# Attention slots in another order: scores one slot sooner, one queued item a slot, quotients ahead of copies and weight casts

## The chip, the core and the metric

The kernel runs on one core of a Trainium2 chip. The time is the device time of one execution, in microseconds (us). Five engines each work through their own list of instructions in order and signal one another by semaphores: TensorE (PE in the profile, its weight loads as PEld), VectorE (DVE), ScalarE (ACT), GpSimd (POOL) and SyncE (SP), which here only issues DMAs.

## The reference

A decoder trunk of two layers over 512 tokens of width 1024, in float32: a recurrent layer, a dense feed-forward layer (SwiGLU), an attention layer, a second SwiGLU. Only the attention layer matters here:

```python
def attention_layer(x, norm_g, w_qkv, q_norm, k_norm, w_out):
    b, l, _ = x.shape
    h = rmsnorm(x, norm_g)
    qkv = (h @ w_qkv).reshape(b, l, 3, ATT_HEADS, ATT_HEAD_DIM)
    pos = jnp.arange(l, dtype=jnp.float32)
    q = partial_rope(rmsnorm(qkv[:, :, 0], q_norm), pos) * (ATT_HEAD_DIM ** -0.5)
    k = partial_rope(rmsnorm(qkv[:, :, 1], k_norm), pos)
    v = qkv[:, :, 2]
...
    for window, dilation in DILATED_PATTERNS:
        o_i, m_i, d_i = dilated_window_attention(q, k, v, window, dilation)
...
    wts = jnp.stack(dens) * jnp.exp(m_all - jnp.max(m_all, axis=0, keepdims=True))
    o = jnp.sum(wts[..., None] * jnp.stack(outs), axis=0) / jnp.sum(wts, axis=0)[..., None]
    o = o.astype(x.dtype).reshape(b, l, ATT_WIDTH)
    return x + o @ w_out
```

There are 16 heads of 64 channels. The three window patterns, merged by their softmax denominators, amount to one softmax over scores to which the logarithm of how many patterns see the key is added; the kernel holds that table in `lnc`.

## The kernel before

Every float32 matrix is split into two parts, `hi` (a cast on ScalarE, line 89) and `lo` (the remainder, a subtraction on VectorE, line 90), and a product is three matmuls. A weight block of 128 x 1024 comes by one DMA on SP's queue into one of three raw buffers, is split by `weight_emit`, and is used two blocks later.

The attention layer is written as two streams that one hand-written order weaves together (`manual_schedule`: the four compute engines keep the order in which the code emits). The first stream is a list of `pieces`, each six matmuls of 512 columns or twelve of 256, some 1.4 us of TensorE. A group g of four heads has 16 pieces for queries and keys (`qk_pieces`) and 8 for values (`v_pieces`); then come 16 pieces of the output projection for each half of the heads (`ao_pieces`). The last four query and key pieces of a group are followed by `finish_a` (copy out of PSUM and square on ScalarE), `finish_b` (sum of squares on VectorE, a power on GpSimd), `finish_c` (scaling), `finish_d` and `finish_e` (rotary part).

The second stream is the attention of eight pairs of heads, 0 to 7, each in twelve slots, 0 to 11. For a head, `turn(h, b)` transposes a block of probabilities into PSUM and splits it (`ph` on ScalarE, `pl` on VectorE), and `values(h, b)` multiplies it into the one output buffer `po`; b is 0, 1, 2. After `values(h, 2)` ScalarE copies half of `po` to `bot` and VectorE adds both halves into `o` (`add`), which frees `po`; after a pair's second head `o` is split for the output projection. For the next pair, `pair_T` transposes queries and keys (`qk_hi`, `qk_lo`), and `scores(p + 1, b)` makes three sets of scores. Each set is reduced with a custom VectorE instruction (line 885), goes through the exponential on ScalarE (line 886), then `quotients`: a reciprocal of the sums on VectorE (line 891) and a product per block on GpSimd (line 893). `turn(h, 0)` reads all blocks of a head's probabilities, so it needs the quotients of all three sets. Transposes, scores and probabilities share three PSUM buffers (tag `pm`); pieces have four of their own (`pa`).

After the steps of a slot, `fill_in` runs the pieces of that slot. Inside a piece the weight split of a later block and the copy out of PSUM are emitted at once. After each piece `tick` runs those finishing steps that are due by a count of pieces. Only then come the functions in `after_piece`: `quotients` and `add`.

## Time and profile before

| | us |
|---|---|
| median of 3 runs | 1377.83 (1377.36 to 1377.85) |
| profiled execution | 1378.62 |
| its span | 1376.8 |
| attention stage, first projection to last output piece | 718 to 1017 |
| pair 0 begins | 772.9 |
| pairs 1 to 7 begin their first full turn | 804.4, 833.3, 864.6, 894.1, 925.3, 945.7, 970.4 |
| last values of pair 7 | 984.2 |

TensorE is busy for 97% of the span. A matmul's row gives its start and a modelled duration, longer than the distance to the next start, since matmuls overlap. A wait stands in brackets at the end of a row, with the instruction that ended it. The granted clock is the share of TensorE's full speed that the throttle let through.

### The profile page before, as it was taken

How to read it: one execution, taken by the hardware profiler on the slowest of the kernel's cores; microseconds unless marked ns; L12 is line 12 of the kernel's file. 1: busy time of each engine (PE TensorE's matmuls, PEld its weight loads, DVE VectorE, ACT ScalarE, POOL GpSimd, SP SyncE). 2: the span in 40 equal slices, each digit the busy share in tenths (PEclk: the TensorE clock that was granted, in tenths of full speed). 3: DMA queues.
4: the chain of work that ended last, by engine and by line, in shares of the span. 5: the costliest groups of instructions: out<-in, count | busy, mean ns of one | idle time of the engine just before them, and what ended most of it. 6: DMA issues, size and time to landing. Idle time of an engine off the chain costs nothing.

```text
span 1376.8 us, 16001 instructions
## 1 busy us (share of the span) xinstructions
PE 1331.5 (97%) x6314; PEld 1091.1 (79%) x6314; DVE 781.3 (57%) x1264; ACT 553.9 (40%) x818; POOL 75.9 (6%) x94
## 2 busy tenths in 40 slices
PE   8999989999999999999999989888899999999998
PEld 6877767788888888888888877676688888888887
DVE  7877799875544344444465566575564444444442
ACT  6643857443323223223343646464452222222221
POOL 0000000000000000000002314131000000000000
PEclk9999999999999999999999999998999999999999
DMA  6322223532333333333232211110123323333322
GB/s 234 108 92 77 93 77 107 152 93 92 92 101 99 92 96 99 94 97 104 82 102 92 62 53 56 49 59 31 46 92 95 104 92 94 102 88 100 107 88 81
DMA packets 38555, 126.53 MB, mean 92 GB/s; under 512 B 4288, under 2 KB 5056, under 8 KB 38352
## 3 DMA queue, kind: packets, MB, share of 16 engines
q1 hardware_dynamic: 38480, 125.51, 29.5%
q8 instruction: 49, 0.80, 0.2%
q14 instruction: 26, 0.21, 0.1%
HBM read 123.36 MB, written 2.13 MB: 91 GB/s over the span
## 4 chain that ended last, share of the span: by engine, by line
PE 88%; DVE 5%; ACT 5%; issue 1%; POOL 0%; DMA 0%; SPq 0%; ACTq 0%; POOLq 0%; DVEq 0%
PE ps_pr L118 24%; PE ps_pr L119 24%; PE ps_pr L120 23%; PE ps_qkv L763 2%; PE ps_qkv L764 2%; PE ps_qkv L765 2%; ACT s L886 1%; PE ps_pT L901 1%; DVE wl L90 1%; PE ps_ao L118 1%; ACT wh L89 1%; PE ps_ao L119 1%; PE ps_ao L120 1%; PE ps_s L874 1%; PE ps_o L916 1%
## 5 line engine op out<-in xcount | busy, mean ns | idle before, releaser
L89 ACT CAST wh<-wr 128x1024 fp32r<-128x1024 f32 (+2 forms) x223 | 227.9, 1023 | 589.2 <-PE ps_pr L120 386.3
L118 PE MATMUL ps_pr<-xh,wl 128*128 128x512 f32 x1056 | 416.9, 395 | 12.4 <-DVE wl L90 12.0
L119 PE MATMUL ps_pr<-xl,wh 128*128 128x512 f32 x1056 | 414.8, 393 | 0.0
L120 PE MATMUL ps_pr<-xh,wh 128*128 128x512 f32 x1056 | 413.6, 392 | 0.0
L90 DVE TENSOR_TENSOR wl<-wr,wh 128x1024 fp32r<-128x1024 f32 (+2 forms) x223 | 265.1, 1190 | 86.1 <-ACT wh L89 85.3
L118 PEld LDWEIGHTS ps_pr<-xh,wl 128*128 128x128 f32 x1056 | 199.6, 189 | 55.4 <-DVE wl L90 12.9
L119 PEld LDWEIGHTS ps_pr<-xl,wh 128*128 128x128 f32 x1056 | 199.6, 189 | 42.9 <-DVE xl L193 1.3
L120 PEld LDWEIGHTS ps_pr<-xh,wh 128*128 128x128 f32 x1056 | 199.6, 189 | 42.4 <-issue 0.7
L118 PE MATMUL ps_pr<-ah,wl 128*128 128x512 f32 x352 | 136.9, 389 | 0.0
L119 PE MATMUL ps_pr<-al,wh 128*128 128x512 f32 x352 | 136.9, 389 | 0.0
L120 PE MATMUL ps_pr<-ah,wh 128*128 128x512 f32 x352 | 136.9, 389 | 0.0
L672 DVE TENSOR_TENSOR tu<-ps_pr,nrb 128x512 f32<-128x512 f32 x44 | 30.4, 691 | 130.7 <-PE ps_pr L120 130.7
L680 DVE TENSOR_TENSOR x<-ps_pr,x 128x512 f32<-128x512 f32 x48 | 33.2, 692 | 122.6 <-PE ps_pr L120 122.6
L670 DVE TENSOR_TENSOR tg<-ps_pr,nrb 128x512 f32<-128x512 f32 x44 | 30.4, 691 | 94.0 <-PE ps_pr L120 94.0
L120 PEld LDWEIGHTS ps_pr<-ah,wh 128*128 128x128 f32 x352 | 66.1, 188 | 13.8
L119 PEld LDWEIGHTS ps_pr<-al,wh 128*128 128x128 f32 x352 | 66.1, 188 | 13.7
L118 PEld LDWEIGHTS ps_pr<-ah,wl 128*128 128x128 f32 x352 | 66.1, 188 | 13.6
L886 ACT ACTIVATE s<-s,m 128x512 f32<-128x512 f32 (+3 forms) x64 | 35.4, 554 | 55.6 <-DVE m L885 42.1
L763 PE MATMUL ps_qkv<-wh,xl 128*128 128x512 f32 x128 | 54.8, 428 | 0.0
L764 PE MATMUL ps_qkv<-wl,xh 128*128 128x512 f32 x128 | 51.2, 400 | 0.0
L765 PE MATMUL ps_qkv<-wh,xh 128*128 128x512 f32 x128 | 51.1, 400 | 0.0
L901 PE MATMUL ps_pT<-cst,s 128*128 128x128 f32 x160 | 30.1, 303 | 19.3 <-POOL s L893 19.2
(230 smaller groups left out, 1633.6 us busy)
## 6 DMA issues: line engine op xcount, KB each, us to landing
wr<-in_w_gu SPq DMA_DIRECT2D x88, 512.0 KB, 3.5
wr<-in_w_in SPq DMA_DIRECT2D x35, 512.0 KB, 3.5
wr<-in_w_dn SPq DMA_DIRECT2D x32, 448.0 KB, 3.3
wr<-in_w_qkv SPq DMA_DIRECT2D x24, 512.0 KB, 3.5
wr<-in_w_out SPq DMA_DIRECT2D x16, 512.0 KB, 3.5
wr<-in_w_dn SPq DMA_DIRECT2D x16, 512.0 KB, 3.5
x<-in_xT SPq DMA_DIRECT2D x16, 256.0 KB, 3.5
bcs<-csd SPq DMA_DIRECT2D x16, 256.0 KB, 4.3
```

The lines of the kernel that those rows point to most:

```text
L89: S.copy(hi, src)
L90: V.tensor_tensor(out=lo, in0=src, in1=hi.bitcast(F32), op=ALU.subtract)
L118: mm(ps, lhsT=wl[ws], rhs=xh[xs], start=start, stop=False)
L119: mm(ps, lhsT=wh[ws], rhs=xl[xs], start=False, stop=False)
L120: mm(ps, lhsT=wh[ws], rhs=xh[xs], start=False, stop=stop)
L670: V.tensor_tensor(out=tg, in0=pg, in1=rb, op=ALU.mult)
L680: V.tensor_tensor(out=x[m], in0=ps, in1=x[m], op=ALU.add)
L763: mm(pss[t], lhsT=xl[:, ts_], rhs=wh[:, cols], start=(k == 0), stop=False)
L764: mm(pss[t], lhsT=xh[:, ts_], rhs=wl[:, cols], start=False, stop=False)
L765: mm(pss[t], lhsT=xh[:, ts_], rhs=wh[:, cols], start=False, stop=(k == KD - 1))
L886: S.activation(s, s, AF.Exp, scale=-1.0, bias=m[:, 0, u:u + 1], accum_out=m[:, 1, u:u + 1])
L901: nc.tensor.transpose(ps[:, c + (i - j) * P:c + (i - j + 1) * P], prob[h, i][:, j * P:(j + 1) * P], ident)
```

## The change

The pieces now lie in one order with all of a group's 24 pieces added before an even pair. `slot_end` replaces `fill_in`: after each piece it runs one function of `queue` (finishing steps, now one at a time, whatever the count), then the functions of `behind` (`quotients`, `add`), then those of `last` (weight splits and copies out of PSUM, which pieces now only register). A slot without a piece does the last three steps alone. The steps of a pair are given by `head_steps`: each values stands two slots behind its turn, the next pair's scores stand in slots 5, 7 and 9 (6, 8 and 10 before), and a pair's last values move into slot 0 of the next pair, in front of its first turn. The pieces given to pairs 0 to 7 are 12, 12, 12, 12, 10, 5, 4, 4 (12, 12, 12, 12, 12, 4, 5, 4 before), 40 instead of 36 pieces run before pair 0, and one is left after pair 7 instead of three.

```diff
-        after_piece = []
-
-        def later(n, f):
-
-            queue.append([n, f])
-
-        def tick():
-            for e in queue:
-                e[0] -= 1
-            due = [e for e in queue if e[0] <= 0]
-            queue[:] = [e for e in queue if e[0] > 0]
-            for _, f in due:
-                f()
+        behind, last = [], []
...
                 if t == 2:
-                    weight_emit(i + AHEAD)
+                    last.append(lambda: weight_emit(i + AHEAD))
                 if kp == 3:
-                    finish_a(t)
+                    last.append(lambda: finish_a(t))
...
-                later(2, lambda: finish_b(t, sq))
-                later(6, lambda: finish_c(t))
+                queue.append(lambda: finish_b(t, sq))
                 if t == NT - 1:
-                    later(7, finish_d)
-                    later(8, finish_e)
+                    for u in range(NT):
+                        queue.append(lambda u=u: finish_c(u))
+                    queue.extend(finish_d + [finish_e])
...
-            after_piece.append(quotients)
+            behind.append(quotients)
...
-            after_piece.append(add)
+            behind.append(add)
...
-        def fill_in(n=1):
-            for _ in range(min(n, len(pieces))):
-                pieces.pop(0)()
-                tick()
-            ready = after_piece[:]
-            after_piece.clear()
-            for f in ready:
+        def slot_end(n=1):
+
+            for _ in range(max(n, 1)):
+                if n:
+                    pieces.pop(0)()
+                if queue:
+                    queue.pop(0)()
+                for fs in (behind, last):
+                    ready = fs[:]
+                    fs.clear()
+                    for f in ready:
+                        f()
+
+        def head_steps(p):
+
+            ha, hb = 2 * p, 2 * p + 1
+            steps = [
+                [lambda: turn(ha, 0)],
+                [lambda: pair_T(p + 1, 0)],
+                [lambda: values(ha, 0), lambda: turn(ha, 1)],
+                [lambda: pair_T(p + 1, 1)],
+                [lambda: values(ha, 1), lambda: turn(ha, 2)],
+                [lambda: scores(p + 1, 0)],
+                [lambda: values(ha, 2), lambda: turn(hb, 0)],
+                [lambda: scores(p + 1, 1)],
+                [lambda: values(hb, 0), lambda: turn(hb, 1)],
+                [lambda: scores(p + 1, 2)],
+                [lambda: values(hb, 1), lambda: turn(hb, 2)],
+                [],
+            ]
+            if p == 7:
+                steps = [fs if k % 2 == 0 else [] for k, fs in enumerate(steps)]
+            if p > 0:
+                steps[0].insert(0, lambda: values(ha - 1, 2))
+            return steps
...
-                n = [12, 12, 12, 12, 12, 4, 5, 4][p]
-                nxt = p < 7
-                ha, hb = 2 * p, 2 * p + 1
-                steps = [
-                    [lambda: turn(ha, 0)],
-                    [lambda: turn(ha, 1)] + ([lambda: pair_T(p + 1, 0)] if nxt else []),
-                    [lambda: values(ha, 0), lambda: turn(ha, 2)],
-                    [lambda: values(ha, 1)] + ([lambda: pair_T(p + 1, 1)] if nxt else []),
-                    [lambda: values(ha, 2)],
-                    [lambda: turn(hb, 0)],
-                    [lambda: scores(p + 1, 0)] if nxt else [],
-                    [lambda: values(hb, 0), lambda: turn(hb, 1)],
-                    [lambda: scores(p + 1, 1)] if nxt else [],
-                    [lambda: values(hb, 1), lambda: turn(hb, 2)],
-                    [lambda: scores(p + 1, 2)] if nxt else [],
-                    [lambda: values(hb, 2)],
-                ]
-                for k, fs in enumerate(steps):
+                n = (12, 12, 12, 12, 10, 5, 4, 4)[p]
+                for k, fs in enumerate(head_steps(p)):
                     for f in fs:
                         f()
-                    fill_in(n * (k + 1) // 12 - n * k // 12)
-            fill_in(len(pieces))
+                    slot_end(n * (k + 1) // 12 - n * k // 12)
+            values(15, 2)
+            slot_end(len(pieces))
```

Three places show what this does to the lists of the engines. The first is VectorE at the end of pair 0, from the reduction of the next pair's last scores (`s,m<-ps_s`) to its reciprocal (`m<-m`); `wl` is the low part of a weight, `v` a value block, `q<-rc,rs` the rotary sum, `pl` the low part of turned probabilities. Before:

```order
L885 ISA s_6157,m_6156<-ps_s_6148,cst_82 128x256
L885 ISA m_6156 128x1
L885 ISA s_6160,m_6156<-ps_s_6149,cst_82 128x256
L885 ISA m_6156 128x1
L90 TENSOR_TENSOR wl133_6177<-wr133_6175,wh133_6176 128x1024
L838 SCALAR_TENSOR_TENSOR v_6181<-ps_v_6023,nrt_5431,v_6181 128x4x64
L807 TENSOR_TENSOR q_5685<-rc_6144,rs2_6145 128x32x8
L808 TENSOR_TENSOR q_5685<-rc_6144,rs2_6145 128x32x8
L891 RECIPROCAL m_6156<-m_6156 128x2
L838 SCALAR_TENSOR_TENSOR v_6204<-ps_v_6058,nrt_5431,v_6204 128x4x64
```

Now:

```order
L878 ISA s_6197,m_6196<-ps_s_6188,cst_82 128x256
L878 ISA m_6196 128x1
L878 ISA s_6200,m_6196<-ps_s_6189,cst_82 128x256
L878 ISA m_6196 128x1
L884 RECIPROCAL m_6196<-m_6196 128x2
L90 TENSOR_TENSOR pl_6220<-ps_pT_6216,ph_6219 128x256
L90 TENSOR_TENSOR wl134_6231<-wr134_6229,wh134_6230 128x1024
```

The weight's low part, a value block and the rotary sums stood between the reduction and the reciprocal; nothing stands there now.

The second is ScalarE at the end of pair 1, around the exponentials of the last scores (128x256 x2); `q` and `qsq` are `finish_a`, `ph` and `wh` are casts of probabilities and of a weight, `bot` the copy out of `po`. Before:

```order
L89 CAST ph_6417<-ps_pT_6414 128x256
L886 ACTIVATE s_6436,m_6435<-s_6436,m_6435 128x256
L886 ACTIVATE s_6439,m_6435<-s_6439,m_6435 128x256
L89 CAST wh136_6449<-wr136_6448 128x1024
L924 COPY bot_6302<-ps_o_6356 64x512
L89 CAST xh9_6467<-o_6301 128x512
L89 CAST ph_6476<-ps_pT_6471 128x512
L774 ACTIVATE q_6225<-ps_qkv_6221,nrt_5431 128x512
L776 ACTIVATE qsq_6487<-q_6225 128x512
```

Now:

```order
L764 ACTIVATE qsq_6441<-q_6179 128x512
L879 ACTIVATE s_6452,m_6451<-s_6452,m_6451 128x256
L879 ACTIVATE s_6455,m_6451<-s_6455,m_6451 128x256
L762 ACTIVATE q_6179<-ps_qkv_6176,nrt_5431 128x512
L764 ACTIVATE qsq_6471<-q_6179 128x512
L89 CAST ph_6480<-ps_pT_6477 128x256
L89 CAST wh137_6494<-wr137_6493 128x1024
L762 ACTIVATE q_6179<-ps_qkv_6177,nrt_5431 128x512
L764 ACTIVATE qsq_6500<-q_6179 128x512
L762 ACTIVATE q_6179<-ps_qkv_6178,nrt_5431 128x512
L764 ACTIVATE qsq_6512<-q_6179 128x512
L917 COPY bot_6362<-ps_o_6422 64x512
```

Four copies with their squares, which came after the next pair's first turn (the first of them is the last two rows of the list before), now surround the exponentials and stand ahead of `bot`; the list begins with the square of the first, whose copy stands just ahead.

The third is VectorE at the end of pair 5, in the pairs with few pieces; `x` is an addition of the output projection, and the 128x256 `pl` is the last split of the pair. Before:

```order
L90 TENSOR_TENSOR pl_7590<-ps_pT_7586,ph_7589 128x256
L885 ISA s_7602,m_7601<-ps_s_7593,cst_82 128x256
L885 ISA m_7601 128x1
L885 ISA s_7605,m_7601<-ps_s_7594,cst_82 128x256
L885 ISA m_7601 128x1
L891 RECIPROCAL m_7601<-m_7601 128x2
L951 TENSOR_TENSOR x1_1905<-ps_ao_7570,x1_1905 128x512
L927 TENSOR_TENSOR o_7489<-ps_o_7533,bot_7490 64x512
```

Now:

```order
L90 TENSOR_TENSOR pl_7593<-ps_pT_7587,ph_7592 128x512
L878 ISA s_7605,m_7604<-ps_s_7596,cst_82 128x256
L878 ISA m_7604 128x1
L878 ISA s_7608,m_7604<-ps_s_7597,cst_82 128x256
L878 ISA m_7604 128x1
L884 RECIPROCAL m_7604<-m_7604 128x2
L90 TENSOR_TENSOR wl147_7622<-wr147_7620,wh147_7621 128x1024
L946 TENSOR_TENSOR x2_1947<-ps_ao_7572,x2_1947 128x512
L90 TENSOR_TENSOR pl_7635<-ps_pT_7631,ph_7634 128x256
L90 TENSOR_TENSOR pl_7654<-ps_pT_7648,ph_7653 128x512
L920 TENSOR_TENSOR o_7534<-ps_o_7584,bot_7535 64x512
```

The last split stood ahead of the scores; it now stands behind them, behind a weight's low part and behind an addition, and `o` stands behind the first split of the next pair instead of ahead of it.

## Rows read from the trace of the kernel before

**Rows 1.** The page: span, and each engine's busy time, share and instructions.

```profile
span 1376.8 us, 16001 instructions
PE 1331.5 (97%) x6314; PEld 1091.1 (79%) x6314; DVE 781.3 (57%) x1264; ACT 553.9 (40%) x818; POOL 75.9 (6%) x94
```

**Rows 2.** What TensorE waited for between 718 and 1017 us: waiting line, releaser, us in total, times, longest.

```profile
PE ps_pT L901 <- POOL s L893: 19.2, 7, 5.2
PE ps_o L916 <- DVE pl L90: 7.6, 7, 2.4
PE ps_s L874 <- DVE m L885: 1.6, 2, 1.4
```

**Rows 3.** Busy time by stretch, one row per pair (pair 0 to 7 without pair 4): stretch, its length, busy us and instructions of PE, PEld, DVE, ACT and POOL, granted clock, DMA share, GB/s.

```profile
772.90:804.36 31.46, 26.20 (x190) 23.13 (x188) 22.04 (x52) 19.15 (x41) 13.02 (x14) 0.96 0.21 54
804.36:833.00 28.64, 27.65 (x140) 21.82 (x140) 14.50 (x34) 13.47 (x30) 3.81 (x8) 0.92 0.16 52
833.00:864.57 31.57, 26.08 (x189) 23.14 (x189) 23.02 (x54) 19.77 (x42) 12.92 (x14) 0.98 0.19 54
864.57:893.80 29.23, 28.20 (x140) 22.31 (x140) 14.53 (x34) 13.47 (x30) 3.86 (x8) 0.90 0.16 51
...
925.33:946.00 20.67, 18.31 (x95) 14.44 (x96) 12.84 (x34) 11.70 (x28) 4.49 (x9) 0.84 0.13 48
946.00:970.40 24.40, 19.05 (x98) 14.48 (x96) 13.22 (x34) 11.59 (x28) 3.80 (x9) 0.86 0.07 21
970.40:984.60 14.20, 11.42 (x54) 8.81 (x55) 7.74 (x12) 5.13 (x9) 0.38 (x1) 0.88 0.12 38
```

**Rows 4.** TensorE's timeline where pairs 1 to 5 begin, and two waits in pairs 5 and 6: start, duration, line, operation, form; in brackets the wait ahead of it.

```profile
804.36 0.90 PE L901 MATMUL ps_pT<-cst,s 128*128 128x128 f32 x3 [5.11 <-POOL s L893]
...
809.03 0.47 PE L763 MATMUL ps_qkv<-wh,xl 128*128 128x512 f32 x1
...
833.32 0.55 PE L901 MATMUL ps_pT<-cst,s 128*128 128x128 f32 x3 [1.30 <-POOL s L893]
...
835.88 0.47 PE L763 MATMUL ps_qkv<-wh,xl 128*128 128x512 f32 x1
...
864.57 0.90 PE L901 MATMUL ps_pT<-cst,s 128*128 128x128 f32 x3 [5.17 <-POOL s L893]
...
894.08 0.55 PE L901 MATMUL ps_pT<-cst,s 128*128 128x128 f32 x3 [1.30 <-POOL s L893]
...
925.33 1.76 PE L901 MATMUL ps_pT<-cst,s 128*128 128x128 f32 x7 [5.16 <-POOL s L893]
...
936.74 0.32 PE L874 MATMUL ps_s<-qk_lo,qk_hi 64*128 64x128 f32 x1 [1.35 <-DVE m L885]
...
948.72 0.72 PE L916 MATMUL ps_o<-pl,v 128*128 128x512 f32 x1 [1.66 <-DVE pl L90]
```

**Rows 5.** The timelines of TensorE, VectorE, ScalarE and GpSimd between the last scores of pair 0 and the first turn of pair 1, columns as before.

```profile
795.48 0.28 PE L874 MATMUL ps_s<-qk_hi 64*128 64x256 f32 x2
...
798.79 0.41 DVE L885 CUSTOM_DVE_ANT_0 s<-ps_s,cst 128x256 f32<-128x256 f32 x1
...
801.30 1.23 DVE L90 TENSOR_TENSOR wl<-wr,wh 128x1024 fp32r<-128x1024 f32 x1 [1.75 <-ACT wh L89]
...
803.50 0.16 DVE L891 RECIPROCAL m<-m 128x2 f32<-128x2 f32 x1
...
800.24 1.03 ACT L89 CAST wh<-wr 128x1024 fp32r<-128x1024 f32 x1
...
803.83 0.93 POOL L893 TENSOR_SCALAR s<-s,m 128x256 f32<-128x256 f32 x2 [4.03 <-DVE m L891]
```

**Rows 6.** The same chain at the end of pair 5, from TensorE's last scores to the first turn of pair 6, with one piece of the output projection between 943.69 and 945.08.

```profile
942.64 0.28 PE L874 MATMUL ps_s<-qk_hi 64*128 64x256 f32 x2
...
943.69 0.39 PE L118 MATMUL ps_ao<-xh,wl 128*128 128x512 f32 x1
...
945.08 0.27 PE L901 MATMUL ps_pT<-cst,s 128*128 128x128 f32 x1
945.65 0.55 PE L901 MATMUL ps_pT<-cst,s 128*128 128x128 f32 x3 [0.30 <-POOL s L893]
...
943.21 0.42 DVE L885 CUSTOM_DVE_ANT_0 s<-ps_s,cst 128x256 f32<-128x256 f32 x1
...
945.11 0.93 POOL L893 TENSOR_SCALAR s<-s,m 128x256 f32<-128x256 f32 x2 [1.08 <-DVE m L891]
```

**Rows 7.** The copy of a `finish_a` on ScalarE and the first instruction after its square, and one power on GpSimd.

```profile
840.06 0.69 ACT L774 ACTIVATE q<-ps_qkv,nrt 128x512 f32<-128x512 f32 x1
...
841.32 0.67 ACT L853 ACTIVATE qk_hi<-ps_qT,gain 128x512 fp32r<-128x512 f32 x1
...
839.39 1.65 POOL L787 TENSOR_TENSOR qrs<-qss,mhalf 128x8 f32<-128x8 f32 x1 [5.67 <-DVE qss L786]
```

**Rows 8.** Pair 7, from the last values of its first head (they end at about 977.4) to the first values of its second.

```profile
977.58 0.58 ACT L924 COPY bot<-ps_o 64x512 f32<-64x512 f32 x1 [1.60 <-PE ps_o L917]
...
978.19 0.68 DVE L927 TENSOR_TENSOR o<-ps_o,bot 64x512 f32<-64x512 f32 x1 [0.36 <-ACT bot L924]
...
978.80 0.69 DVE L90 TENSOR_TENSOR pl<-ps_pT,ph 128x512 fp32r<-128x512 f32 x1
...
979.55 0.51 PE L916 MATMUL ps_o<-pl,v 128*128 128x512 f32 x1 [0.18 <-DVE pl L90]
```

More of the change, by code (lines that the diff above doesn't have):

```diff
@@ L796, in views, with rotate @@
                 return q, c, s
-            def finish_d():
-                sqs["rc"] = at.tile([P, NT, 8, 16], F32, tag="rc", name="rc", bufs=1)
-                sqs["rs2"] = at.tile([P, NT, 8, 16], F32, tag="rs", name="rs2", bufs=1)
-                q, c, s = views()
-                V.tensor_tensor(out=c, in0=q[:, :, 0:16], in1=cc.rearrange("p t h e -> p (t h) e"), op=ALU.mult)
-                V.tensor_tensor(out=s, in0=q[:, :, 0:16], in1=sc.rearrange("p t h e -> p (t h) e"), op=ALU.mult)
+            def rotate(key, tag, tab):
+                sqs[key] = at.tile([P, NT, 8, 16], F32, tag=tag, name=tag, bufs=1)
+                q = qk[g].rearrange("p t h e -> p (t h) e")
+                out = sqs[key].rearrange("p t h e -> p (t h) e")
+                V.tensor_tensor(out=out, in0=q[:, :, 0:16], in1=tab.rearrange("p t h e -> p (t h) e"), op=ALU.mult)
+            finish_d = [lambda: rotate("rc", "rc", cc), lambda: rotate("rs2", "rs", sc)]
             def finish_e():
@@ L831, in piece, with finish_v @@
                 if t == 2:
-                    weight_emit(i + AHEAD)
+                    last.append(lambda: weight_emit(i + AHEAD))
                 if vp == 1:
-                    v = ap_.tile([P, 4, 2, 64], F32R, tag=f"v{t}", name="v", bufs=2)
-                    r = norm.rt[:, t:t + 1]
-                    pv3 = ps.rearrange("p (h e) -> p h e", h=4)
-                    S.activation(v[:, :, 0], pv3, AF.Copy, scale=r)
-                    V.scalar_tensor_tensor(out=v[:, :, 1], in0=pv3, scalar=r, in1=v[:, :, 0].bitcast(F32), op0=ALU.mult, op1=ALU.subtract)
-                    vt[g, t] = v
+                    last.append(lambda: finish_v(t))
+            def finish_v(t):
+                ps = pss[t][:, :256]
+                v = ap_.tile([P, 4, 2, 64], F32R, tag=f"v{t}", name="v", bufs=2)
+                r = norm.rt[:, t:t + 1]
+                pv3 = ps.rearrange("p (h e) -> p h e", h=4)
+                S.activation(v[:, :, 0], pv3, AF.Copy, scale=r)
+                V.scalar_tensor_tensor(out=v[:, :, 1], in0=pv3, scalar=r, in1=v[:, :, 0].bitcast(F32), op0=ALU.mult, op1=ALU.subtract)
+                vt[g, t] = v
             return [lambda vp=vp, t=t: piece(vp, t) for vp in range(2) for t in range(NT)]
@@ L947, in piece, with add_x @@
                 if m2 == 0 and kk == 1:
-                    weight_emit(i + AHEAD)
+                    last.append(lambda: weight_emit(i + AHEAD))
                 if kk == 1:
-                    m = 2 * mp + m2
-                    V.tensor_tensor(out=x[m], in0=st["ps"], in1=x[m], op=ALU.add)
-                    if after is not None:
-                        after(m)
+                    last.append(lambda ps=st["ps"]: add_x(2 * mp + m2, ps))
+            def add_x(m, ps):
+                V.tensor_tensor(out=x[m], in0=ps, in1=x[m], op=ALU.add)
+                if after is not None:
+                    after(m)
@@ L969, in trunk @@
         with tc.manual_schedule(engines=ORDERED):
             pieces += qk_pieces(0)
-            fill_in(4)
+            slot_end(4)
             norm.finish()
-            fill_in(12)
-            pieces += v_pieces(0)
-            fill_in(8)
-            pieces += qk_pieces(1)
-            fill_in(2)
-            pair_T(0, 0)
-            pair_T(0, 1)
-            fill_in(3)
-            for b in range(3):
-                scores(0, b)
-                fill_in(2)
-            fill_in(1)
+            slot_end(12)
@@ L985, in trunk @@
+            pieces += v_pieces(0) + qk_pieces(1)
+            slot_end(11)
+            for f in (lambda: pair_T(0, 0), lambda: pair_T(0, 1), lambda: None, lambda: scores(0, 0), lambda: scores(0, 1), lambda: scores(0, 2)):
+                f()
+                slot_end(2)
+            slot_end(1)
             for p in range(8):
@@ L988, in trunk @@
                     pieces += v_pieces(g + 1)
[L989 to L1010 removed]
+                    pieces += qk_pieces(g + 2) if g < 2 else ao_pieces(0)
+                n = (12, 12, 12, 12, 10, 5, 4, 4)[p]
+                for k, fs in enumerate(head_steps(p)):
                     for f in fs:
                         f()
[L1013 to L1014 removed]
+                    slot_end(n * (k + 1) // 12 - n * k // 12)
+            values(15, 2)
+            slot_end(len(pieces))
             assert not queue
             pieces += ao_pieces(1, norm3.feed)
[L1017 removed]
+            slot_end(len(pieces))
     def store(m):
```

6 lines of the change are left out of this document (removed).

## The prediction

> **What bounds the kernel now.** I read the page first, then the granted clock and busy time by stretch, then TensorE's waits, and last the timelines of all engines around each wait. The span is one long TensorE program [rows 1]; the change touches only the attention stage, 718 to 1017 us. There TensorE's waits sum to 19.2 + 7.6 + 1.6 = 28.4 us [rows 2], so whatever this edit can give lies in those 28.4 us and in what the clock loses after them. The reader is to see that no other engine is full there: in pair 0 VectorE works 22.0 of 31.5 us and ScalarE 19.2 [rows 3]. What costs time is the order in which four in-order engines hand work round.
>
> Three waits of 5.11, 5.17 and 5.16 us stand where pairs 1, 3 and 5 begin, and two of 1.30 us where pairs 2 and 4 begin [rows 4]; all are the first turn of a pair waiting for the quotients of its last scores. The first: those scores leave TensorE at about 795.75; VectorE reduces them only at 798.79; its reciprocal, which needs exponentials that end at about 800.3, starts at 803.50, because a weight split stands ahead of it that waits for its cast (800.24, 1.03 us) and runs 1.23 us; GpSimd starts at 803.83 [rows 5]. With nothing in the way the same chain took 942.9 to 945.65, 2.7 us [rows 6].
>
> After each long wait the clock is at half. Eleven transposes and one piece take 809.03 - 804.36 = 4.67 us at pair 1 and 835.88 - 833.32 = 2.56 at pair 2, after only 1.30 us of waiting: 2.1 us lost [rows 4].
>
> The five waits hold 18.0 us, which leaves 28.4 - 18.0 = 10.4 us for the thin pairs 5 to 7, where 13 pieces stand in 36 slots and the granted clock is 0.84 to 0.88 [rows 2 to 4].
>
> **Part 1: scores a slot sooner, quotients first (pairs 0 to 4).** No instruction is added or dropped on the path; everything is order. Between the last scores and the next pair's first turn now stand three pieces, two values and a short turn. A piece is 945.08 - 943.69 = 1.39 us [rows 6], so the cover is 3 x 1.39 + 1.0 = 5.2 us (two pieces and one short values before, 3.0 us). The free chain needs 2.7, so 2.5 us of queued work fits under it. I followed the new order with the durations of the rows, starting the pair's first scores at zero:
>
> - Pairs 0 and 2 (value pieces in slots 0 to 7). The split of slot 6 (wh 0.95, wl 1.14 between starts) and two value copies push the reduction of the second scores to 7.05, their exponentials end at 9.4, the probability split of slot 8 at 10.95. TensorE wants that at 10.3: a wait of 0.65, and 0.1 for a score buffer. The last reciprocal is then at 12.5, the quotient at 13.3, and TensorE arrives at 14.75. So 5.11 becomes 0.75, twice.
> - Pair 4 lacks a piece in slots 0 and 6 and has value copies in slots 5, 7, 8, 9: 0.95 (values waiting for the head's sum) + 0.7 (last values) = 1.7 in place of 5.16.
>
> Removed: 15.4 us of waits, 2.6 of the two 1.30s, and half clock three times, 6 us in all: 24.0. Added in their place: 0.75 + 0.75 + 1.7 = 3.2. Bounds of this part: if the backlog is nil, 0 is added; if the waits merely shrink by the one slot (1.4 us) and the 1.8 us that the weight split costs, 5.1 becomes 2, three times, and nothing is gained on the clock: 6 us added and 6 kept.
>
> **Part 2: the query and key copies now fall into the end of pairs 1 and 3.** Four of them (a copy and a square, 841.32 - 840.06 = 1.26 us of ScalarE each [rows 7]) moved from slots 0 to 3 of the even pairs to slots 8 to 11 of the odd ones. Behind them on ScalarE wait the exponentials, the short cast, the copy `bot` and the first cast of the next pair; on GpSimd a power of 1.65 us [rows 7] stands ahead of the last quotients. By the rows, the quotient is ready at 12.95 against TensorE's 13.7: no wait. But ScalarE is booked until about 16.8, then come the split (0.6), one reduction (0.75) and the head's sum (0.65): 18.9, and TensorE wants the single output buffer at 17.7. That is 1.2 us at pair 2; at pair 4, whose slot 0 has no piece, 1.2 + 1.4 = 2.65. With 1.5 us of half clock after the second: 5.4 us. Bounds: 0 (ScalarE 1.2 us ahead of my count) and 2 x 5.2 with 2.1 of clock each, 14.6, if the power and the copies delay the quotients as the weight split does now.
>
> **Part 3: the thin pairs 5 to 7.** Here the new order is the worse one. Before, head A's turns ran two ahead of its values; now each values stands two slots behind its turn, and with one piece or none between. Three things follow.
>
> - Last values and the next turn share a slot, so ScalarE does `bot`, then the cast, VectorE the split, then the sum that frees the one output buffer. Where the sum stood before the split, 977.4 to 979.55 went by [rows 8]; now the buffer is free about 2.75 us after the last values, and TensorE has a turn (0.5) and perhaps a transpose (0.4) to do. I get 2.5 (a weight split stands before it), 1.65 and 2.0 for the first heads and 0.55, 1.3 and 2.1 for the second.
> - A weight split and an addition of 0.7 us stand ahead of the last probability split in pair 5 (2.6), ahead of the last scores' reduction in pair 6 (0.6 + 2.25), and in pair 7 (0.3).
> - Score buffers, key splits: 1.4 in pair 5, 0.7 in pair 6.
>
> Together 7.05 + 6.5 + 4.4 = 18, against 10.4: +7.5 us, and 1 us for one more stretch at half clock. Bounds: -2 (no split comes late, and the first heads wait no longer than the 1.66 us of pair 6 now [rows 4]) and +16 (8.5 us of half clock instead of 1). I take 8.5.
>
> The clock first by rows: 1.30 us of waiting left it at full (pair 2's piece ran at the full 2.4 GHz level), 1.35 and 1.66 us were followed by the 1.2 GHz level, 0.84 and 0.86 granted over those stretches [rows 3, 4]. Beside this stands the Trainium skill, page "TensorE: Matmul & The Clock Gate", section "A second HAM failure mode: psum-queue depth-cycling": a kernel whose matmul groups are parted by many small idles has its clock swing between both levels and loses throughput. The rows of the thin pairs agree. By that rule trading three long waits for many of 1 to 2.6 us gives no gain: that is rival C.
>
> **Edits at nothing.** The weight DMAs keep their one queue and their order; SP issues them ahead through three raw buffers, and no wait of TensorE above names a transfer. If that cover went, a late cast would cost its 1.03 us per weight. Moving copies behind quotients delays PSUM buffers by under a slot, with three slots before reuse. One queued item a slot spreads the same VectorE work. After pair 7 one piece instead of three covers the last sum: 0.3 us.
>
> **Sum.** -24.0 + 3.2 + 5.4 + 8.5 + 0.3 = -6.6 us. The profiled execution took 1378.62 (span 1376.8 and 1.8 around it), so 1372.0; the runs' median lies 0.8 lower, so I forecast 1371.
>
> **Rivals.**
> A, the tail costs nothing: pieces and engines absorb part 3, as VectorE is busy only 12.84 of 20.67 us in pair 5 [rows 3]. Against it: those are latencies, not load. -15.1 us: 1363.
> B, slower: the copies of part 2 act as the weight split did. It decides from the point where the last reciprocal or GpSimd's power comes over 5.2 us after the last scores. Price 14.6 instead of 5.4, and 1.5 us in each of pairs 0 to 4 for values late by the same backlog: -6.6 + 9.2 + 7.5 = +10: 1388. For it: my margin at pair 2 is 0.75 us over some ten queued instructions.
> C, no gain: eight stops of 1.3 us or more in the thin pairs each cost up to the 2.1 us of half clock, 8 more than before instead of 1: +0.4: 1378.
> D, the order moves but the waits only change their name, so that part 1 keeps 12 of its 24: with the rest as forecast, 1371 + 9 = 1380.
>
> **Chances.** Forecast (1366 to 1375) 0.50, A 0.22, C 0.13, B 0.08, D 0.07. What a measurement of this kernel can tell is about 0.2%, 2.8 us: faster below 1375.1, slower above 1380.6. The forecast with A gives 0.72 and a bit of C 0.02: faster 0.74; most of C and half of D make same 0.14; slower 0.12. For 8 in 10 the range reaches from A to where C and D lie: 1361 to 1380.
>
> **What would show it.** Right: no wait over 2 us for quotients where pairs 1, 3 and 5 begin, granted clock 0.99 or more over pairs 0 to 3, waits of 1 to 3 us on the split or the sum at the first values of pairs 2, 4, 5, 6, 7, and a longer stretch from pair 5's first turn to the last values (59.3 us now). Part 1 is wrong if the reciprocal of the last scores still starts over 2 us after its exponentials; part 2 if pair 2 starts with a wait on GpSimd; part 3 if the thin pairs take 59 us or less. A time under 1361 would mean I overcount latencies, one above 1380 that the backlog moved.

## The result, and the profile after

The changed kernel took 1369.37 us (median of 4 runs, 1368.61 to 1369.81) where the kernel before took 1377.84 (4 runs, 1377.36 to 1378.76): a ratio of 0.9937, 95% interval 0.992 to 0.9954. It is faster by 0.6%. The profiled execution took 1369.81 us, 8.8 less than that of before, and its span is shorter by the same 8.8 us.

The page after, which answers to [rows 1]: the same 16001 instructions, and every engine's busy time within 4 us of before. Nothing was saved in work; the 8.8 us are waiting, gaps and clock.

```profile
span 1368.0 us, 16001 instructions
PE 1327.8 (97%) x6314; PEld 1088.4 (80%) x6314; DVE 782.9 (57%) x1264; ACT 554.0 (40%) x818; POOL 75.2 (5%) x94
```

TensorE's waits of the attention stage after, with the columns of [rows 2] (waiting line, releaser, us in total, times, longest). L909 is the first values matmul (L916 before), L920 the sum of a head (L927 before), L90 a split.

```profile
PE ps_o L909 <- DVE o L920: 16.1, 9, 2.8
PE ps_o L909 <- DVE pl L90: 5.6, 6, 2.4
PE ps_s L867 <- DVE qk_lo L847: 0.5, 1, 0.5
PE ps_s L867 <- DVE m L878: 0.3, 1, 0.3
```

The line that led the list before, turns waiting for GpSimd's quotients (19.2 us, 7 times), is gone altogether. In its place stands one that was not in the list: values waiting for the sum `o` that frees the one output buffer, 16.1 us. In total 22.5 us stand where 28.4 stood. That is 5.9 us less of waiting; the remaining 2.9 of the 8.8 must come from the clock and from gaps that the view counts as no wait.

Where they stand, by pair, with the columns of [rows 3]. A stretch goes from a pair's first turn to the next pair's; the last ends just after the last values of pair 7.

```profile
779.10:805.37 26.27, 25.95 (x189) 23.04 (x188) 21.64 (x48) 16.01 (x36) 10.21 (x12) 1.00 0.19 61
805.37:830.72 25.35, 25.35 (x143) 20.19 (x142) 15.21 (x38) 16.57 (x36) 6.20 (x10) 1.00 0.21 63
830.72:858.82 28.10, 26.33 (x190) 23.18 (x189) 22.23 (x50) 16.72 (x37) 9.55 (x11) 1.00 0.19 58
858.82:884.18 25.36, 25.36 (x143) 20.20 (x142) 15.22 (x38) 16.56 (x36) 6.20 (x10) 1.00 0.20 63
884.18:911.97 27.79, 23.58 (x178) 20.88 (x177) 21.43 (x50) 16.56 (x37) 9.55 (x11) 1.00 0.18 57
911.97:936.71 24.74, 18.99 (x100) 14.21 (x99) 15.03 (x35) 11.56 (x28) 4.16 (x8) 0.91 0.08 24
936.71:961.11 24.40, 18.60 (x93) 14.40 (x93) 13.40 (x33) 11.56 (x28) 5.01 (x8) 0.81 0.12 42
961.11:980.50 19.39, 14.72 (x66) 11.69 (x65) 8.01 (x12) 6.38 (x11) 0.12 (x1) 0.82 0.04 8
```

Two halves can be read off it. In pairs 0 to 4 the granted clock is 1.00 throughout (0.90 to 0.99 before), and in pairs 1 and 3 TensorE is busy for the whole stretch, 25.35 of 25.35 and 25.36 of 25.36 us. In pairs 5 to 7 the clock is 0.81 to 0.91 and TensorE idles for 16 us.

To compare like with like, pieces have to be counted, since the change also hands them out differently. A piece is 1.39 us [rows 6].

- Pairs 0 to 4: 132.9 us (779.10 to 911.97) against 152.4 (772.90 to 925.33), with 58 pieces against 60. Without the two pieces (2.8) the gain is 16.7 us.
- Pair 5's first turn to the end of pair 7's last values: 67.8 us (911.97 to 979.80) against 59.3, that is +8.5. But one more piece lies in it, since pair 7's last values now stand behind the piece of slot 11: +7.1 like for like.
- Ahead of pair 0: 6.2 us later, with four more pieces (5.6): +0.6. As much, 0.7 us, stands there already when the attention stage begins (718.95 against 718.24), where the two kernels are the same.
- After the last values: 388.2 us against 392.2, with three pieces fewer (4.2): +0.2.

Together -16.7 + 7.1 + 0.6 + 0.2 = -8.8 us, the difference of the spans.

TensorE's timeline after, at the places of [rows 4], same columns: the first turns of pairs 1 to 4, the first values behind those of pairs 2 and 4, and three later waits, with the turn between the last two.

```profile
805.37 0.60 PE L894 MATMUL ps_pT<-cst,s 128*128 128x128 f32 x4
...
830.72 0.60 PE L894 MATMUL ps_pT<-cst,s 128*128 128x128 f32 x4
...
836.01 0.47 PE L909 MATMUL ps_o<-pl,v 128*128 128x512 f32 x1 [1.40 <-DVE o L920]
...
858.82 0.60 PE L894 MATMUL ps_pT<-cst,s 128*128 128x128 f32 x4
...
884.18 0.60 PE L894 MATMUL ps_pT<-cst,s 128*128 128x128 f32 x4
...
889.47 0.47 PE L909 MATMUL ps_o<-pl,v 128*128 128x512 f32 x1 [2.83 <-DVE o L920]
889.78 0.39 PE L910 MATMUL ps_o<-ph,v 128*128 128x512 f32 x1
...
915.23 0.67 PE L909 MATMUL ps_o<-pl,v 128*128 128x512 f32 x1 [2.22 <-DVE o L920]
...
936.12 0.58 PE L909 MATMUL ps_o<-pl,v 128*128 128x256 f32 x1 [2.35 <-DVE pl L90]
...
936.71 1.05 PE L894 MATMUL ps_pT<-cst,s 128*128 128x128 f32 x4
...
940.01 0.77 PE L909 MATMUL ps_o<-pl,v 128*128 128x512 f32 x1 [1.39 <-DVE o L920]
```

None of the four turns has a bracket: where 5.11, 1.30, 5.17 and 1.30 us stood, TensorE does not stop. The new waits of pairs 2 and 4 come behind that turn and two pieces (pair 2) or one (pair 4), where the values need the output buffer.

The chain of [rows 5] after, at the end of pair 0, from TensorE's last scores (first row) over VectorE's reduction, ScalarE's exponentials and VectorE's reciprocal to GpSimd's quotients; ScalarE's weight cast and VectorE's split of that weight follow.

```profile
799.25 0.39 PE L867 MATMUL ps_s<-qk_hi 64*128 64x256 f32 x2
...
801.39 0.41 DVE L878 CUSTOM_DVE_ANT_0 s<-ps_s,cst 128x256 f32<-128x256 f32 x1
...
802.97 0.17 DVE L884 RECIPROCAL m<-m 128x2 f32<-128x2 f32 x1 [0.82 <-ACT s L879]
...
804.19 1.23 DVE L90 TENSOR_TENSOR wl<-wr,wh 128x1024 fp32r<-128x1024 f32 x1 [0.53 <-ACT wh L89]
...
802.75 0.19 ACT L879 ACTIVATION_READ_ACCUMULATOR s<-s,m 128x1 f32 x1
...
803.10 1.05 ACT L89 CAST wh<-wr 128x1024 fp32r<-128x1024 f32 x1
...
803.23 0.94 POOL L886 TENSOR_SCALAR s<-s,m 128x256 f32<-128x256 f32 x2 [1.16 <-DVE m L884]
```

The reciprocal now starts as the exponentials end (802.94) and the weight's split comes 1.2 us behind it; before, it started 3.2 us after the exponentials, behind that split. GpSimd is done at 804.17, and TensorE, which has three pieces and two values in between, comes to the turn only at 805.37.

And the end of pair 1, where the query and key copies now lie: GpSimd's power and quotients, ScalarE's last copy with its square, the copy `bot` and the cast, VectorE's reciprocal, the next split, the reduction of a square and the sum.

```profile
827.51 1.65 POOL L775 TENSOR_TENSOR qrs<-qss,mhalf 128x8 f32<-128x8 f32 x1 [0.61 <-DVE qss L774]
829.15 0.94 POOL L886 TENSOR_SCALAR s<-s,m 128x256 f32<-128x256 f32 x2
...
831.08 0.67 ACT L762 ACTIVATE q<-ps_qkv,nrt 128x512 f32<-128x512 f32 x1
831.78 0.63 ACT L764 ACTIVATE qsq<-q 128x512 f32<-128x512 f32 x1
832.43 0.58 ACT L917 COPY bot<-ps_o 64x512 f32<-64x512 f32 x1
833.04 0.59 ACT L89 CAST ph<-ps_pT 128x512 fp32r<-128x512 f32 x1
...
827.50 0.17 DVE L884 RECIPROCAL m<-m 128x2 f32<-128x2 f32 x1
...
833.66 0.69 DVE L90 TENSOR_TENSOR pl<-ps_pT,ph 128x512 fp32r<-128x512 f32 x1 [1.49 <-ACT ph L89]
834.27 0.68 DVE L773 TENSOR_REDUCE qss<-qsq 128x8 f32<-128x512 f32 x1
...
835.18 0.69 DVE L920 TENSOR_TENSOR o<-ps_o,bot 64x512 f32<-64x512 f32 x1
```

The quotients wait for the power (ready 827.67, started 829.15) and are done at 830.09, 0.6 us ahead of the turn at 830.72. `bot`, though `po` was complete at about 830.9, waits for the copies until 832.43; then cast, split, a reduction and the sum follow one another, and the values that need the buffer start at 836.01, 1.40 us late.

### The profile page after: what moved, and what is told of

It reads as the page before. It is cut to its first block, busy times and chain, and to the rows that moved or that the text cites. A ratio compares the mean times of both kernels' runs of the same rounds, so it can differ in the third digit from the quotient of the medians.

```text
span 1368.0 us, 16001 instructions
## 1 busy us (share of the span) xinstructions
PE 1327.8 (97%) x6314; PEld 1088.4 (80%) x6314; DVE 782.9 (57%) x1264; ACT 554.0 (40%) x818; POOL 75.2 (5%) x94
## 4 chain that ended last, share of the span: by engine, by line
PE 87%; ACT 6%; DVE 4%; issue 2%; POOL 1%; DMA 0%; SPq 0%; POOLq 0%; ACTq 0%; DVEq 0%
PE ps_pr L118 24%; PE ps_pr L119 24%; PE ps_pr L120 24%; ACT s L879 2%; PE ps_qkv L751 2%; PE ps_qkv L753 2%; PE ps_qkv L752 2%; PE ps_ao L118 1%; PE ps_ao L120 1%; PE ps_ao L119 1%; PE ps_pT L894 1%; PE ps_o L909 1%; PE ps_v L819 1%; PE ps_v L818 1%; PE ps_v L817 1%
## 5 line engine op out<-in xcount | busy, mean ns | idle before, releaser
L90 DVE TENSOR_TENSOR wl<-wr,wh 128x1024 fp32r<-128x1024 f32 (+2 forms) x223 | 265.5, 1191 | 63.3 <-ACT wh L89 62.3
L90 DVE TENSOR_TENSOR pl<-ps_pT,ph 128x512 fp32r<-128x512 f32 (+1 forms) x48 | 28.8, 601 | 32.7 <-ACT ph L89 32.3
```

The costliest lines, as they stand in the source:

```text
L90: V.tensor_tensor(out=lo, in0=src, in1=hi.bitcast(F32), op=ALU.subtract)
```

## The experiments

All ratios are against the kernel before, run on the same chip; the changed kernel stands at 0.9937. Every kernel here computes the whole reference. Two theories were on trial. For pairs 0 to 4: that scores a slot sooner *and* quotients ahead of the casts end the long waits, or that one of the two does it alone. For pairs 5 to 7: that the new order of steps costs 7 to 8 us there, or that the few pieces do, whatever the order.

**1. Quotients behind the casts again.** They go into a third list, run behind `last`.

```diff
-            behind.append(quotients)
+            quots.append(quotients)
...
-                for fs in (behind, last):
+                for fs in (behind, last, quots):
```

> The changed kernel (1369.4 us) with the quotients put behind the copies and weight casts of their slot again; the sum of the heads stays where it is. Theory (the gain comes from the scores standing a slot sooner, in a slot without a weight split, so that the reciprocal has nothing long ahead of it in either order): 1369 to 1372, no wait for quotients over 1 us where pairs 1 to 5 begin. Rival (it is the rank of the quotients that gives the gain): 1375 or more, waits of 2 us or more for quotients where pairs 1, 3 and 5 begin.

Measured 1368.82 us (1367.97 to 1370.44, 5 runs), 0.9932 [0.992, 0.9944]: the same as the changed kernel, just under the expected band, with no wait for quotients anywhere. With the scores in slots 5, 7 and 9 the quotients' place in the lists is worth nothing.

**2. Scores a slot later again.** Slots 6, 8 and 10 in every pair, all else as changed.

```diff
-                [lambda: scores(p + 1, 0)],
-                [lambda: values(ha, 2), lambda: turn(hb, 0)],
+                [],
+                [lambda: values(ha, 2), lambda: turn(hb, 0), lambda: scores(p + 1, 0)],
```

(and so for slots 8 and 10)

> The changed kernel with the three score sets one slot later (slots 6, 8, 10, as before), all else as changed. Theory: the cover falls from 5.2 to about 3.0 us against a chain of 2.7 and 1 to 2 us of queued work, so waits for quotients of about 1 us come back at five pair starts: 1372 to 1377. Rival (rank alone matters): 1369 to 1371, no such waits.

Measured 1378.23 us (1374.29 to 1380.14, 12 runs), 0.9999 [0.9989, 1.001]: the whole gain is gone, about a microsecond more than I expected. Yet pairs 1 and 3 begin without a wait. The new waits stand elsewhere; the turn on TensorE, the reduction of its last scores on VectorE, then GpSimd, at the end of pair 1 of this kernel:

```profile
832.08 0.55 PE L894 MATMUL ps_pT<-cst,s 128*128 128x128 f32 x3 [2.86 <-POOL s L886]
...
827.87 0.41 DVE L878 CUSTOM_DVE_ANT_0 s<-ps_s,cst 128x256 f32<-128x256 f32 x1
...
829.52 1.64 POOL L775 TENSOR_TENSOR qrs<-qss,mhalf 128x8 f32<-128x8 f32 x1 [0.86 <-DVE qss L774]
831.14 1.33 POOL L886 TENSOR_SCALAR s<-s,m 128x256 f32<-128x256 f32 x2
```

The reduction starts 2.0 us after the scores have left TensorE (825.9), behind a square's reduction and a split that waits for ScalarE's query and key copies. Then a power of 1.64 us stands ahead of the quotients, as it does in the changed kernel, but here no margin is left, and the pair's turn waits 2.86 us; the same at pair 4, and 0.71, 1.68 and 1.62 where pairs 5, 6 and 7 begin. By stretches, pairs 1 to 4 take 112.8 us (803.71 to 916.51; 106.6 in the changed kernel) and pairs 5 to 7 3.4 us more. So with the pieces as they now lie the earlier slot is needed at pairs 2 and 4 and in the thin pairs, not at pairs 1 and 3.

**3. Both undone.** Experiments 1 and 2 in one kernel. (The expectation speaks of the sums too; as in experiment 1, only the quotients go behind the casts.)

> The changed kernel with both parts of the reordering that the earlier runs undid one at a time: scores in slots 6, 8 and 10 again, and the quotients and sums behind the casts and copies again. Theory: at pairs 1 and 3 either part alone was enough, so undoing both brings back waits for quotients of 2 us or more where pairs 1, 3 and 5 begin, and longer ones than 2.9 us at pairs 2 and 4: 1383 to 1395. Rival: the new order of the pieces (and one queued item a slot) keeps pairs 1 and 3 free by itself, and the quotients' place matters nowhere: under 1380, with no wait of 2 us at pairs 1 and 3.

Measured 1384.15 us (1380.74 to 1384.79, 6 runs), 1.0035 [1.0022, 1.0047]: slower than the kernel before. Pairs 1 and 3 wait again, 1.63 and 2.06 us, pairs 2 and 4 3.30 and 3.31; pair 5 waits 0.69, where I had expected 2. Its chain at the end of pair 0, TensorE, VectorE, ScalarE and GpSimd:

```profile
800.33 0.28 PE L867 MATMUL ps_s<-qk_hi 64*128 64x256 f32 x2
...
805.53 0.55 PE L894 MATMUL ps_pT<-cst,s 128*128 128x128 f32 x3 [1.63 <-POOL s L886]
...
801.01 0.41 DVE L878 CUSTOM_DVE_ANT_0 s<-ps_s,cst 128x256 f32<-128x256 f32 x1
...
803.53 1.22 DVE L90 TENSOR_TENSOR wl<-wr,wh 128x1024 fp32r<-128x1024 f32 x1 [1.75 <-ACT wh L89]
804.67 0.16 DVE L884 RECIPROCAL m<-m 128x2 f32<-128x2 f32 x1
...
802.46 1.03 ACT L89 CAST wh<-wr 128x1024 fp32r<-128x1024 f32 x1
...
805.00 0.93 POOL L886 TENSOR_SCALAR s<-s,m 128x256 f32<-128x256 f32 x2 [2.47 <-DVE m L884]
```

This is the picture of [rows 5] again: a reciprocal of 0.16 us behind a split that waits for its cast. So at pairs 1 and 3 either part is enough alone. But the wait is 1.63, not 5.11: the reduction starts 0.4 us after the last scores end, where it took 3.0 us before. That part the other edits give: the new order of the pieces, the one queued item a slot, or the casts and copies that now come behind that item. No run here parts these.

**4. The place of quotients and sums alone, in the kernel before.** Old steps, old pieces, old queue; only the casts, copies and additions are put behind the quotients and sums. (The sums move with the quotients here; no wait of TensorE before was for a sum [rows 2]. The counts of the finishing steps are one lower, so that they fall due after the same piece.)

```diff
                 if t == 2:
-                    weight_emit(i + AHEAD)
+                    last.append(lambda: weight_emit(i + AHEAD))
                 if kp == 3:
-                    finish_a(t)
+                    last.append(lambda: finish_a(t))
```

(and so for the value copies and the additions of the output projection)

> The kernel before (1377.8 us) with one part of the change alone: weight casts, copies out of PSUM and additions of a piece are emitted behind the quotients and sums of their slot; steps, pieces and finishing steps as before. Theory (the reciprocal behind the weight split cost 3.2 us of each 5.1 us wait and all of the 1.3 us ones; the tail stays as it was): waits of about 2 us at pairs 1, 3 and 5, less half clock, 1361 to 1367, so faster than the whole change. Rival (without the slot the waits only change their name): 1374 to 1378.

Measured 1360.28 us (1359.94 to 1360.81, 4 runs), 0.9869 [0.9856, 0.9882]. One idea of the change, alone, is worth twice the whole change. Its waits (line numbers of that kernel: L906 turn, L921 values; a third row of 1.6 us is left out), and from TensorE's timeline the longest of them:

```profile
PE ps_o L921 <- DVE pl L90: 13.0, 10, 3.6
PE ps_pT L906 <- POOL s L898: 4.2, 5, 1.2
...
910.66 0.79 PE L921 MATMUL ps_o<-pl,v 128*128 128x512 f32 x1 [3.58 <-DVE pl L90]
```

The 19.2 us for quotients are 4.2, the longest 1.2. Pairs 0 to 4 take 133.4 us (772.22 to 905.65) with the same 60 pieces, 19.0 less than before, at a granted clock of 1.00. Pairs 5 to 7 take about what they took (60.2 us against 59.3), but not with the same waits: at pair 5 the 5.16 us for quotients became 1.17, and 3.58 us for the split of its first values (the last row) stand behind them in its place.

**5. The old steps in pairs 5 to 7 only**, the rest as changed; pair 7's last values stand in slot 11 again.

```diff
+            if p >= 5:
+                steps = [
+                    [lambda: turn(ha, 0)],
+                    [lambda: turn(ha, 1), lambda: pair_T(p + 1, 0)],
+                    [lambda: values(ha, 0), lambda: turn(ha, 2)],
...
-            if p > 0:
+            if 0 < p < 6:
```

> The changed kernel with pairs 5 to 7 in the steps of the kernel before (two turns ahead of the values, scores in slots 6, 8, 10, last values in slot 11); pieces per pair and the rank of quotients as changed. Theory (the thin pairs lose 8 us by the order of their steps): 1359 to 1364, 58 to 61 us from pair 5's first turn to the last values instead of 67.8. Rival (they lose it by where pieces and weight splits fall, or by the clock): 1367 or more, 65 us or more.

Measured 1360.27 us (1359.64 to 1360.67, 4 runs), 0.9868 [0.9855, 0.9881]: 0.7% below the changed kernel, some 9 us. The number of pieces is the same, so with these pieces the order of steps is what costs there. From pair 5's first turn to the start of the last values it takes 58.4 us (910.40 to 968.75) where the changed kernel takes 67.4 (911.97 to 979.39, with the one piece more): 7.7 us without that piece. The rest of the 9 us lies ahead of the attention stage, which this execution reached 1.5 us sooner, and is no gain of the edit. The waits of 1.40 and 2.83 us at pairs 2 and 4 stay.

**6. The sum ahead of the next turn's split.** The commonest releaser after is `o`, which comes behind the split of the turn that follows the values. Here its addition is issued with the values.

```diff
+            V.tensor_tensor(out=o[rows], in0=po[:64], in1=bot[rows], op=ALU.add)
+
             def add():
-                V.tensor_tensor(out=o[rows], in0=po[:64], in1=bot[rows], op=ALU.add)
                 if e == 1:
```

> The changed kernel with VectorE's sum of a head (the one that frees the output buffer) emitted right behind its values, ahead of the next turn's split; its later split stays where it was. Theory (nine waits, 16.1 us, end with that sum, and it stands one split too late): each becomes 0.6 to 0.7 us shorter, 10 to 11 us in all, and a little half clock goes: 1361 to 1365. Rival (the first values then wait for the split of their own turn, which ends as late): 1368 to 1370, the waits only change their releaser.

Measured 1359.77 us (1359.03 to 1360.57, 4 runs), 0.9865 [0.9852, 0.9879], a larger gain than expected. The longest row of its waits (two below it hold 0.8 and 0.3 us):

```profile
PE ps_o L909 <- DVE pl L90: 14.2, 11, 2.3
...
```

All nine waits for `o` are gone, the one at pair 2 altogether; at pair 4 1.19 us are left, now for the split. The two instructions have changed places on VectorE: TensorE waits 16.1 us less for the sum and 8.6 more for the split that now comes second.

**7. Pieces handed out as before** (36 ahead of pair 0; 12, 12, 12, 12, 12, 4, 5, 4), the new steps kept.

```diff
-                n = (12, 12, 12, 12, 10, 5, 4, 4)[p]
+                n = (12, 12, 12, 12, 12, 4, 5, 4)[p]
```

(and so for the pieces ahead of pair 0)

> The changed kernel with the pieces handed out as before (36 before pair 0; 12, 12, 12, 12, 12, 4, 5, 4), so that the four query and key copies fall into slots 0 to 3 of pairs 2 and 4 again. Theory (those copies hold ScalarE when pairs 2 and 4 begin): the waits of 1.4 and 2.8 us there go, value copies in slots 8 to 11 of pairs 0, 2 and 4 cost less than 1 us: 1364 to 1368. Rival (the sum is late for another reason): the two waits stay within 0.5 us, 1369 or more.

Measured 1361.91 us (1361.08 to 1363.87, 4 runs), 0.9883 [0.9869, 0.9896]: the new handing out costs some 7 us, more than expected. With the query and key copies back in slots 0 to 3 of the even pairs, the waits of 1.40 and 2.83 us are gone: pairs 0 to 4 take 131.7 us (772.89 to 904.60), 3.9 less than the changed kernel with the same 60 pieces (132.9 + 2.8). The other half was not foreseen: pairs 5 to 7 take 64.2 us (904.60 to 968.80) where the changed kernel takes 67.8 with as many pieces. So of the 7 us that the new steps cost there, the old pieces take back half, and the old steps (experiment 5) all.

**8. That, with scores a slot later** (7 and 2 together).

> The changed kernel with pieces handed out as before (36 ahead of pair 0; 12, 12, 12, 12, 12, 4, 5, 4) and scores in slots 6, 8 and 10 again. Theory: the later slot costs only where copies, squares and the power of a query and key group stand at the end of an odd pair, so with the pieces as before the waits of 2.86 us for quotients at pairs 2 and 4 go, and the loss against pieces as before alone (1361.9) is that of the thin pairs, 2 to 5 us: 1363 to 1368. Rival: the slot costs there whatever the pieces are, 9.4 us again: 1370 to 1373, with waits of 2 us or more for quotients at two of pairs 1 to 4.

Measured 1362.79 us (1360.76 to 1364.27, 4 runs), 0.9884 [0.987, 0.9897], level with 7 and just under the expected band. No turn of pairs 1 to 5 waits for quotients (0.80 and 1.26 us at pairs 6 and 7). So the earlier slot, worth 9 us in 2, is worth nothing once the pieces lie as before and the quotients come first: here it pays only for a collision that the new handing out makes.

**9. More pieces for the thin pairs** (12, 11, 11, 11, 8, 7, 6, 5).

> The changed kernel with 5 pieces moved from pairs 1 to 4 to pairs 5 to 7 (12, 11, 11, 11, 8, 7, 6, 5). Theory (the thin pairs wait on latencies that any work would cover): 3 to 6 us less, 1363 to 1366. Rival (pairs 1 to 4 have as little to spare, so the waits move there): 1368 to 1371.

Measured 1362.75 us (1361.73 to 1363.96, 4 runs), 0.9887 [0.9873, 0.99], just under the expected band. The clock over the run rose from 0.99 to 0.994, though pair 2 now waits 3.34 us where it waited 1.40.

**10. Old steps in pairs 5 to 7 and the early sum** (5 and 6 together).

> The changed kernel with pairs 5 to 7 in their old steps and a head's sum ahead of the next turn's split. Theory: the old steps already part the last values from the next turn in pairs 5 to 7, so the early sum gives only what it gives at pairs 2 and 4 (1.40 and 2.83 us now, 0 and 1.2 then): 1356 to 1359. Rival: the early sum pushes splits back everywhere by its 0.65 us and gives nothing where the old steps stand: 1359.5 to 1362.

Measured 1357.47 us (1354.61 to 1358.39, 4 runs), 0.9842 [0.9829, 0.9856], as expected. Of the 0.72% that the early sum gave in 6, 0.26% is left where the old steps stand: in pairs 5 to 7 the two mend much the same.

**11. Experiment 4 with pieces 12, 12, 12, 12, 11, 6, 6, 5.**

> The kernel before with quotients first (the one of 1360.3 us) and 4 pieces more in pairs 5 to 7, one from pair 4 and three from behind pair 7 (12, 12, 12, 12, 11, 6, 6, 5). Theory (waits of 13.8 us in the thin pairs, of which four pieces of 1.4 us cover two to four): 1356 to 1359. Rival (those pieces stand where nothing waits): 1360 to 1361.

Measured 1356.83 us (1353.58 to 1357.53, 5 runs), 0.9836 [0.9823, 0.985], as expected: 0.33% below experiment 4.

**12. The early sum and the spread pieces in the changed kernel** (6 and 9 together).

> The changed kernel with two edits together: pieces 12, 11, 11, 11, 8, 7, 6, 5 for pairs 0 to 7, and a head's sum ahead of the next turn's split. Theory: in the thin pairs the two remove different waits (spreading gives TensorE work while a split comes, the early sum frees the output buffer), so most of both gains (6.6 and 9.6 us) adds up: 1354 to 1358. Rival: both remove the same waits, those for the output buffer, and the second gives little: 1358.5 to 1361.

Measured 1353.02 us (1351.38 to 1355.7, 4 runs), 0.9816 [0.9802, 0.9829], just under the expected band, below both kernels and, by its median, every other variant. Its waits:

```profile
PE ps_o L909 <- DVE pl L90: 9.1, 10, 2.8
PE ps_qT L843 <- DVE q L797: 2.8, 1, 2.8
PE ps_s L867 <- DVE qk_lo L847: 0.4, 1, 0.4
```

The two gains add up: 0.72% and 0.50% alone, 1.21% together. 12.3 us of waits are left of 28.4.

## Why the prediction was right, and where its steps were off

The time was forecast as 1371 (a sum of -6.6 us) and came out at 1369.4 (-8.8 in the profiled execution). The signs that it named for being right came: no turn of pairs 1, 3 and 5 waits for quotients, the first values of pairs 2, 4, 5, 6 and 7 wait 1.40, 2.83, 2.22, 1.39 and 2.36 us on the sum, and the stretch of pairs 5 to 7 is longer. By its steps:

**Part 1 (24.0 off, 3.2 back in pairs 0 to 4).** Right. Pairs 1 to 4 begin without a wait, pairs 0 and 2 lose 0.32 and 0.38 us (0.75 forecast) and pair 4 1.00 + 0.38 (0.95 + 0.7). The clock is 1.00, at least the 0.99 that I named. What the forecast did not see is which part does it. It priced "scores a slot sooner, quotients first" as one. Experiments 1 to 3 show that at pairs 1 and 3 either is enough, and 4 and 8 that the quotients' place gives the gain without the slot. What the slot alone would give in the kernel before, no run tried. Experiment 7 prices this part by itself, new steps with the old pieces: 131.7 us against 152.4, -20.7 where -24.0 + 3.2 = -20.8 was forecast; that it agrees so closely is partly luck, as the waits left in it sum to 2.0 us where 3.2 were forecast.

**Part 2 (5.4).** The waits are right: 1.40 against 1.2 and 2.83 against 2.65, at the place and for the reason given (`bot` behind the copies, then the sum behind split and reduction); the margin of the quotients at pair 2 was 0.6 us against 0.75. The 1.5 us of half clock after the second wait was wrong: the values after 2.83 us of waiting ran at full pace (0.47 and 0.39 us at 889.47, where 0.77 and 0.63 is half). Experiment 7 puts this part at 3.9 us in pairs 0 to 4, and shows a price of handing the pieces out anew that the forecast did not have here: 3.6 us in the thin pairs.

**Part 3 (18 of waits, +8.5).** Right in kind, a little large. Pair 5 waits 2.22 + 0.27 + 0.90 + 2.35 = 5.74 us (7.05 forecast), pair 6 1.39 + 0.47 + 1.77 + 0.34 + 1.83 = 5.80 (6.5), pair 7 2.36 + 2.25 = 4.61 (4.4): 16.15 against 18. The score buffers were overcounted, 0.74 us in all where I had 2.1. The stretch of 67.8 us is what 59.3 + 8.5 gives, but partly by luck: I had not counted the piece that moves into it, so the order itself cost 7.1. Experiment 5 shows that it is the order, with the pieces as they now lie (7.7 us by its stretch); experiment 7 shows that with the old pieces the same order costs only 3.5 (64.2 - 1.4 - 59.3). The forecast put the whole on the order.

**The sum.** Like for like, pairs 0 to 4 came to -16.7 where -24.0 + 3.2 + 5.4 = -15.4 was forecast, the thin pairs to +7.1 against +8.5, and the two ends to +0.8 against +0.3. The 2.2 us between forecast and profile are these: 1.3, 1.4 and -0.5.

**The rivals.** A (the tail costs nothing) falls: experiment 5 takes that cost out and gains 7.7 us there. D (waits only change their name) falls for pairs 0 to 4, where they vanish; it is half true of the total, as 16.1 us now stand on a releaser that had no row before. Its price of 9 us holds only if the 3.2 us that part 1 adds are dropped with it; with them it is 12, and 1383. B did not happen, but came near: a power does stand ahead of the last quotients of pair 1, and 0.6 us of margin was left. Experiment 2, with the scores one slot later, has no margin, and the gain is gone. C (many small stops cost the clock) fails by its size: pairs 5 to 7 were granted 0.91, 0.81 and 0.82 after, 0.84, 0.86 and 0.88 before [rows 3], together 0.85 against 0.86. That is by my estimate some 2 us more lost (0.15 of 67.8 us against 0.14 of 59.3), where C needed 8. The rule of the Trainium skill, page "TensorE: Matmul & The Clock Gate", section "A second HAM failure mode: psum-queue depth-cycling", that many small idles make the clock swing, agrees with these three pairs; in pairs 0 to 4, where stops of 0.3 to 2.8 us are many microseconds apart, the granted clock is 1.00.

How the 7.7 us of experiment 5 divide: in pairs 5 to 7 its waits sum to 12.5 us against 16.15, 3.7 less, and the granted clock over the stretch is 0.88 against 0.85, an estimated 3 us (0.12 of 58.4 against 0.15 of 67.4). The last microsecond I have not placed. What stays open besides: the slot alone in the kernel before, and the new order of the pieces and the one queued item a slot, which were not tried apart.

## What to carry to other kernels

Before shifting when a result is produced, look at what stands ahead of its last tiny step on an in-order engine: a reciprocal of 0.16 us started 3.2 us late, behind a cast and a split, where TensorE then waited 5.1 us, and putting quotients and sums first (experiment 4) gave twice what the whole reordering gave. A schedule that is good where filler work is plentiful can be worse where it is thin, so price a new order stage by stage, and undo it where it loses (experiment 5) or mend the one instruction that everything then waits for (experiment 6). When two edits aim at one wait, undo each and both: one may only pay for a collision that another edit makes (experiments 2 and 8).

## What the runs showed of the hardware that I had not expected

The length of a single wait does not tell the clock after it. 2.83 us of waiting at 889.47 was followed by the 2.4 GHz level (0.47 and 0.39 us for the two values), 2.35 us at 936.12 by the 1.2 GHz level: 0.58 us for a form that took 0.39 at 911.63, and 1.05 for the turn at 936.71, which takes 0.60 at 884.18. The 1.39 us at 940.01 fell into that slow stretch and did not begin it. Ahead of the first, TensorE had gone 51 us without a wait above half a microsecond; ahead of the second it had waited 2.22 and 0.90 us in the same pair, the last of them 6 us earlier. In the kernel before, the row at 936.74 does not itself show the level that the prediction reads from it; the matmuls behind it do (0.63 us at 938.85). GpSimd's two quotients took 1.33 us in experiment 2 at 831.14, beside VectorE's split of a weight, and 0.93 to 0.94 in the other rows shown; what slowed them was not tested.
